# VectorE's order in a conv input stage: taps written out by hand, two blocks by turns, thirteen blocks in place of twelve

## The chip, the cores and the metric

The kernel runs on one core of one Trainium2 chip. The metric is the device time of one execution in microseconds. Before the change the median of three executions is 1987.35 us (1987.07 to 1987.43).

## The reference

A trunk of four residual layers over 256 tokens of 2048 features: a causal convolution module, an MLP, a state-space layer, an MLP, and a last RMSNorm. The change touches the first layer alone, up to its LayerNorm:

```
u = rms_norm(x, g) @ w_in + b_in              # (256, 2048) @ (2048, 4096)
a, gate = split(u)
v = a * sigmoid(gate)                         # (256, 2048)
v = depthwise_conv(v, dw, 31 taps, causal) + dw_b
v = silu(layer_norm(v, ln_g, ln_b))           # mean and variance over the 2048 channels
x = x + v @ w_out + b_out
```

## The kernel before

**Layout.** In this stage channels lie on the 128 partitions and the 256 tokens along the free axis. The 2048 channels are 16 blocks of 128, numbered 0 to 15. For each block the loop in `conv_in` multiplies the 2048 input features by the block's 128 value columns and 128 gate columns.

**Matmuls.** Float32 operands are split in a high and a low part. Each weight piece (512 KB, a quarter of a block) is loaded, cast to its high part `hi` on ScalarE (L118), and its low part `lo` is a subtraction (L125), on VectorE for blocks 0 and 1 and on GpSimd for the others (`pool_lo`). `mm_g` then issues 24 matmuls of 256 columns for the quarter (L211 to L213), so a block is 96. `hi` and `lo` have four buffers each: the cast of a quarter waits until TensorE is done with the quarter four before. The accumulators `acc` have two buffers: block c+2 can start when block c's gate is done.

**The gate** (`gate`, L446 to L448), with raised priority: VectorE multiplies the accumulator by the RMSNorm factor (L446, "the gate's multiplication" below), ScalarE takes the sigmoid into `ga` (L447), VectorE forms `(a + b) * ga` into `vT` (L448, "the gate's second instruction").

**The convolution of 31 taps** has two forms.

- Blocks 0 to 11 (`depthwise`): ScalarE computes the first tap into a PSUM bank `cv` (L527), then VectorE adds 30 taps, each one instruction of 128x256 (L829), the last one into `vT`. A tap needs the tap of its block before it. Such a row of taps is called a chain below.
- Blocks 12 to 15, the packed ones (`depthwise_packed`): TensorE does the taps with 32 small matmuls (`pk`, L484) over `R`, a copy of the block shifted four ways. For 12 to 14 ScalarE's queue writes `vT` to DRAM (`vd`) and loads `R` back; for 15 the shifted copies are made by eight copies on VectorE (L470) and eight on ScalarE (L468). VectorE then adds bias and shift (`finish`, L829 `vT<-pk,vecs,shift`). Blocks 12 and 13 run eight quarters after their gates, 14 and 15 after the last block of the stage, in a tail that holds everything up to the first matmul of `conv_out` (L222).

**LayerNorm sums.** Column sums by small matmuls into one bank `stat` (L539). When the first four blocks are convolved, their mean becomes `shift` (a matmul into the bank `mean`, L560, and a VectorE instruction, L562). `centre` then subtracts `shift` from four blocks at once (VectorE, L569, 128x1024) and squares them (ScalarE, L571).

**Banks.** The pool `ms` has four PSUM banks: `cv` of the running chains, `stat`, `mean`, and one in two of the packed sums.

**What sets the order.** A scheduler in the build places the instructions on the five engines, by their place in the program, raised priorities, and its own idea of when operands are ready. On the chip each engine runs its own list strictly in order. `behind(x)` makes the scheduler place one instruction after another. `after(n, f)` calls f some n quarters later. Before the change the taps have no such tie: the scheduler mixes the chains and the gates.

**Beside the stage** GpSimd also builds the packed weights (`wpk`, L386) and adds the output bias to x (L400), for which it loads `bo` itself (L398).

Of the kernel before, what the change touches and what calls it, by code (L numbers as in the profile page):

```python
# [12 lines left out]
AF = mybir.ActivationFunctionType  # L13
ALU = mybir.AluOpType
# [4 lines left out]
P = 128  # L19
EPS = 1e-6  # L20
D = 2048
T = 256
# [7 lines left out]
VW = PAD + T + 2  # L30
NQ = 4
EARLY = 4
PACKED = (12, 13, 14, 15)
URGENT = 300


class Trunk:
# [72 lines left out]
    def split(self, h, urgent=True):  # L110
        i, half = divmod(h, 2)
        raw = self.raws[i] if half == 0 else self.raws.pop(i)
        nk = raw.shape[1] // 2
        sl = raw[:, half * nk:(half + 1) * nk]
        hi = self.w.tile([P, nk] + list(raw.shape[2:]), F32R, tag="hi", name="hi", bufs=4)
        lo = self.w.tile([P, nk] + list(raw.shape[2:]), F32R, tag="lo", name="lo", bufs=4)
        with self.tc.high_priority(offset=URGENT if urgent else 0):
            self.nc.scalar.activation(hi, sl, AF.Copy)  # L118
            eng = self.nc.gpsimd if i in self.pool_lo else self.nc.vector
            if self.barrier is not None and h == 2 * self.barrier + 2:  # L120
                self.low_late = lambda: eng.tensor_tensor(out=lo, in0=sl, in1=hi.bitcast(F32), op=ALU.subtract)
                self.parts[h] = (hi, lo)
                return None
            with self.behind(self.lo_gate) if self.lo_gate is not None else nullcontext():
                ins = eng.tensor_tensor(out=lo, in0=sl, in1=hi.bitcast(F32), op=ALU.subtract)  # L125
            self.lo_gate = None
            if i in self.pool_lo:
                self.pool_ins = ins
            else:
                self.lo_ins = ins  # L130
        self.parts[h] = (hi, lo)
        return ins
# [278 lines left out]
    def conv_in(self):  # L411
        w = self.a["conv_w_in"][0].rearrange("(k p) (h c) -> p k h c", p=P, h=2)
        self.fed = set()
        self.tail = []
        self.stat = None
        st = {}
        for c in range(KB):
            for kc in range(2):
                def consume(hi, lo, half, c=c, kc=kc):
                    if kc == 0 and half == 0:  # L420
                        st["acc"] = self.acc2()
                    A = st["acc"][:, :, 0:T]
                    hi, lo = (t.rearrange("p k h c -> p k (h c)") for t in (hi, lo))
                    self.mm_g([A[:, 0], A[:, 1]], self.hT, hi, lo, kc * 8 + half * 4,
                              kc == 0 and half == 0, kc == 1 and half == 1)
                    if kc == 1 and half == 1:
                        self.gate(c, A)
                if c >= 2:
                    self.pool_lo.add(len(self.steps))
                self.add(w[:, kc * 8:(kc + 1) * 8, :, c * P:(c + 1) * P], [P, 8, 2, P], consume)  # L430
# [10 lines left out]
    def gate(self, c, A):  # L441
        nc = self.nc
        b_in = self.vec("b_in")
        t = self.tmp.tile([P, T], F32, tag="ga", name="ga", bufs=2)
        with self.tc.high_priority(offset=URGENT):
            nc.vector.tensor_tensor(out=A, in0=A, in1=self.rstdB.broadcast_to([P, 2, T]), op=ALU.mult)  # L446
            nc.scalar.activation(t, A[:, 1, :], AF.Sigmoid, bias=b_in[:, KB + c:KB + c + 1])  # L447
            nc.vector.scalar_tensor_tensor(out=self.cblk(c), in0=A[:, 0, :], scalar=b_in[:, c:c + 1], in1=t,  # L448
                                           op0=ALU.add, op1=ALU.mult)
        if c in PACKED:  # L450
            self.depthwise_packed(c)
        else:
            self.depthwise(c)

    def depthwise_packed(self, c):

# [4 lines left out]
        if last:  # L461
            for g in range(4):
                for r in range(4):
                    o = R[32 * r:32 * r + 32, g, :]
                    v = self.vb(c)[32 * g:32 * g + 32, r:r + T + 28]
                    with self.tc.high_priority(offset=URGENT):
                        if r % 2:
                            nc.scalar.activation(o, v, AF.Copy)  # L468
                        else:
                            nc.vector.tensor_copy(out=o, in_=v)  # L470
        else:
            vd = self.dram.tile([P, VW], F32, name=f"vd{i}")
            nc.scalar.dma_start(out=vd, in_=self.vb(c))

            def fetch():
                for r in range(4):
                    nc.scalar.dma_start(out=R[32 * r:32 * r + 32],
                                        in_=vd.rearrange("(g c) t -> c g t", g=4)[:, :, r:r + T + 28])
            self.after(1, fetch)
# [17 lines left out]
                self.colsum(self.stat[:, h, :], (c,), lambda i: v, h == 0)  # L497

        def run():
            ps = self.acc2(f"pk{c}")[:, 0, 0:T] if i % 2 else self.bank([P, T], name=f"pk{c}")  # L500
            products(ps, 0, 5)
            if i:
                feed(c - 1)
# [4 lines left out]
                    self.warm = nc.scalar.activation(warm, R[:, 0, 0:1], AF.Silu)  # L508
            products(ps, 5, 8)
            finish(ps)  # L510
        if i < 2:
            self.after(8, run)
        elif not last:
            self.tail.append(run)
        else:
            while self.pending:
                self.tick()
            for f in self.tail:
                f()
            run()  # L520

    def depthwise(self, c):

        tap = lambda j: (self.vb(c)[:, j:j + T], self.dw[:, c, j:j + 1])
        acc = self.bank([P, T], name="cv")
        v, w = tap(0)
        self.nc.scalar.activation(acc, v, AF.Identity, scale=w, bias=self.vec("dw_b")[:, c:c + 1])  # L527
        for j in range(1, TAPS):
            v, w = tap(j)
            self.stt(self.cblk(c) if j == TAPS - 1 else acc, v, w, acc, ALU.mult, ALU.add)  # L530
        self.ln_feed(c)

# [7 lines left out]
    def ln_feed(self, c):  # L542
        self.fed.add(c)
        if self.stat is None:
            self.stat = self.bank([P, 2, T], name="stat")
        g = range(c // 4 * 4, c // 4 * 4 + 4)
        if not all(i in self.fed for i in g):
            return
        if c < EARLY:
            self.colsum(self.stat[:, 0, :], g, lambda i: self.cblk(g[i]), True)  # L550
            self.after(2, self.ln_shift)
        else:
            self.after(2, lambda: self.centre(g[0], 4))

    def ln_shift(self):
        nc = self.nc
# [2 lines left out]
        ps = self.bank([P, T], name="mean")  # L559
        nc.tensor.matmul(ps, lhsT=self.q4, rhs=t, start=True, stop=True)  # L560
        self.shift = self.const.tile([P, T], F32, name="shift")
        nc.vector.tensor_scalar(out=self.shift, in0=ps, scalar1=1.0 / (EARLY * P), scalar2=None, op0=ALU.mult)  # L562
        for c in range(0, EARLY, 4):
            self.centre(c, 4)

    def centre(self, c, n):
        nc = self.nc
        v = self.cblks(c, n)
        nc.vector.tensor_tensor(out=v, in0=v, in1=self.shift.unsqueeze(1).broadcast_to([P, n, T]), op=ALU.subtract)  # L569
        sq = self.t4([P, n, T], name="sq")  # L570
        nc.scalar.activation(sq, v, AF.Square)  # L571
        cs = range(c, c + n)
# [1035 lines left out]
```

## Time and profile before

| | |
|---|---|
| median of 3 executions | 1987.35 us |
| the profiled execution's own time | 1987.61 us |
| its span, first to last instruction | 1985.8 us |
| TensorE busy | 1966.9 us, 99% |
| VectorE busy | 1401.3 us, 71% |
| ScalarE busy | 952.4 us, 48% |
| GpSimd busy | 274.8 us, 14% |
| the chain that ended last | TensorE 96%, VectorE 2%, DMA 1% |
| mean granted TensorE clock | 0.999 |

Shares are averages over the whole program; the change lies in the first 232 us. Matmuls overlap, so a matmul's duration (0.28 us) is longer than the distance from one to the next. VectorE's instructions overlap too: a tap lasts 0.48 us and the next starts 0.39 us after it.

### The profile page before, as it was taken

Reading aid. Unit: us, or ns where it says so; the run is one execution under the profiler, and the core shown is the slowest. Engines: PE = TensorE matmul, PEld = TensorE weight load, DVE = VectorE, ACT = ScalarE, POOL = GpSimd, SP = SyncE. Lnnn points to the kernel's source line nnn. Section 1 sums busy time; section 2 is a strip of 40 time slices with the busy share of each in tenths; the row PEclk is TensorE's granted clock in tenths of the full one; section 3 lists DMA queues with packets and bytes.
Section 4 is the critical chain, followed back from the end, with each engine's and each line's share of the span. In section 5 each row is a group of like instructions: output and inputs, shape, how many; then the busy total and the mean of one; then the engine's idle time right before and its main releaser. Section 6 shows DMA issues by size and latency. Waiting matters only on the chain.

```text
span 1985.8 us, 28885 instructions
## 1 busy us (share of the span) xinstructions
PE 1966.9 (99%) x11604; PEld 1687.0 (85%) x11604; DVE 1401.3 (71%) x1904; ACT 952.4 (48%) x1179; POOL 274.8 (14%) x252
## 2 busy tenths in 40 slices
PE   8999999999999999999999999999999999999998
PEld 8999788888888888888888788888888888888887
DVE  6899798888787777777558847565555565555655
ACT  6443655544444544444445445454444454444444
POOL 3998300000000221222010000000000000000000
PEclk9999999999999999999999999999999999999999
DMA  8767458667686877877898865665666656565653
GB/s 228 190 184 207 147 183 267 206 226 245 200 260 192 214 229 253 265 246 238 319 308 298 304 215 186 191 191 189 193 190 192 190 191 191 190 213 190 192 191 128
DMA packets 317030, 428.49 MB, mean 216 GB/s; under 512 B 9761, under 2 KB 211553, under 8 KB 313537
## 3 DMA queue, kind: packets, MB, share of 16 engines
q1 hardware_dynamic: 300976, 384.59, 61.6%
q0 software_dynamic: 12352, 37.49, 6.3%
q10 hardware_dynamic: 3568, 4.56, 0.8%
q8 instruction: 91, 1.49, 0.3%
q14 instruction: 43, 0.35, 0.1%
HBM read 400.08 MB, written 34.91 MB: 219 GB/s over the span
## 4 chain that ended last, share of the span: by engine, by line
PE 96%; DVE 2%; DMA 1%; issue 0%; SPq 0%; POOL 0%; ACT 0%; POOLq 0%; DVEq 0%; ACTq 0%
PE acc L199 24%; PE acc L222 15%; PE acc L223 15%; PE acc L224 15%; PE acc L202 12%; PE acc L213 3%; PE acc L212 3%; PE acc L211 3%; PE pk L484 1%; DMA Vt<-Vd 0%; SPq L92 0%; PE kp L1113 0%; PE xw L1254 0%; DMA raw<-in_conv_w_in_dram 0%; PE xt L254 0%
## 5 line engine op out<-in xcount | busy, mean ns | idle before, releaser
L118 ACT ACTIVATE hi<-raw 128x1024 fp32r<-128x1024 f32 x672 | 711.6, 1060 | 953.5 <-PE acc L224 510.2
L125 DVE TENSOR_TENSOR lo<-raw,hi 128x1024 fp32r<-128x1024 f32 x611 | 747.9, 1226 | 505.6 <-ACT hi L118 501.3
L199 PE MATMUL acc<-hT,hi 128*128 128x512 f32 x2048 | 514.4, 393 | 0.0
L199 PEld LDWEIGHTS acc<-hT,hi 128*128 128x128 f32 x2048 | 368.9, 189 | 68.0 <-issue 1.6
L222 PE MATMUL acc<-hi,rT 128*128 128x512 f32 x992 | 387.2, 391 | 0.0
L223 PE MATMUL acc<-lo,rT 128*128 128x512 f32 x992 | 386.4, 390 | 0.0
L224 PE MATMUL acc<-hi,rT 128*128 128x512 f32 x992 | 386.0, 389 | 0.0
L202 PEld LDWEIGHTS acc<-hT,lo 128*128 128x128 f32 x2048 | 279.6, 190 | 20.0
L202 PE MATMUL acc<-hT,lo 128*128 128x256 f32 x2048 | 286.3, 282 | 0.0
L222 PEld LDWEIGHTS acc<-hi,rT 128*128 128x128 f32 x992 | 186.3, 188 | 39.6 <-issue 1.6
L224 PEld LDWEIGHTS acc<-hi,rT 128*128 128x128 f32 x992 | 186.3, 188 | 39.1
L223 PEld LDWEIGHTS acc<-lo,rT 128*128 128x128 f32 x992 | 186.3, 188 | 38.0 <-issue 0.2
L125 POOL TENSOR_TENSOR lo<-raw,hi 128x1024 fp32r<-128x1024 f32 x60 | 143.1, 2402 | 31.3 <-ACT hi L118 24.8
L211 PE MATMUL acc<-hT,hi 128*128 128x256 f32 x512 | 146.1, 286 | 0.9 <-ACT hi L118 0.9
L212 PE MATMUL acc<-hT,hi 128*128 128x256 f32 x512 | 145.7, 286 | 0.3 <-DVE hT L259 0.3
L213 PE MATMUL acc<-hT,lo 128*128 128x256 f32 x512 | 145.5, 286 | 0.0
L829 DVE SCALAR_TENSOR_TENSOR cv<-vT,dw,cv 128x256 f32<-128x256 f32 x348 | 141.3, 486 | 2.2 <-ACT cv L527 1.7
L820 DVE TENSOR_TENSOR x<-x,acc 128x1024 f32<-128x1024 f32 (+1 forms) x72 | 83.6, 1161 | 27.6 <-PE acc L224 22.0
L211 PEld LDWEIGHTS acc<-hT,hi 128*128 128x128 f32 x512 | 98.9, 193 | 3.0 <-issue 1.6
L222 PE MATMUL acc<-hi,yT 128*128 128x512 f32 x256 | 101.1, 395 | 0.0
L212 PEld LDWEIGHTS acc<-hT,hi 128*128 128x128 f32 x512 | 98.8, 193 | 2.2 <-issue 1.6
L223 PE MATMUL acc<-lo,yT 128*128 128x512 f32 x256 | 99.9, 390 | 0.6 <-DVE lo L125 0.6
(285 smaller groups left out, 1722.9 us busy)
## 6 DMA issues: line engine op xcount, KB each, us to landing
raw<-in_mlp_w_up_dram SPq DMA_DIRECT2D x128, 1024.0 KB, 5.8
raw<-in_mlp_w_down_dram SPq DMA_DIRECT2D x128, 1024.0 KB, 5.2
raw<-in_ssm_w_glu_dram SPq DMA_DIRECT2D x32, 1024.0 KB, 5.5
raw<-in_conv_w_in_dram SPq DMA_DIRECT2D x60, 512.0 KB, 5.6
raw<-in_conv_w_out_dram SPq DMA_DIRECT2D x16, 1024.0 KB, 5.2
Vd<-bv POOLq DMA_DIRECT2D x16, 512.0 KB, 6.3
Md<-Kd POOLq DMA_DIRECT2D x32, 256.0 KB, 7.2
Wt<-Wd SPq DMA_DIRECT2D x8, 1024.0 KB, 10.1
```

Source lines behind the costliest of these rows:

```text
L118: self.nc.scalar.activation(hi, sl, AF.Copy)
L125: ins = eng.tensor_tensor(out=lo, in0=sl, in1=hi.bitcast(F32), op=ALU.subtract)
L199: mm(accs[m], lhsT=hi[:, kk, cs[m]], rhs=xT(k0 + kk), start=first and kk == 0, stop=False)
L202: mm(accs[m][:, 0:T], lhsT=lo[:, kk, cs[m]], rhs=xT(k0 + kk)[:, 0, :], start=False, stop=last and kk == 3)
L211: mm(accs[m], lhsT=hi[:, kk, c], rhs=x[:, 0, :], start=first and kk == 0, stop=False)
L212: mm(accs[m], lhsT=hi[:, kk, c], rhs=x[:, 1, :], start=False, stop=False)
L213: mm(accs[m], lhsT=lo[:, kk, c], rhs=x[:, 0, :], start=False, stop=last and kk == 3)
L222: mm(acc[:, b, :], lhsT=ak[:, 0, t], rhs=hi[:, kk, :], start=first and kk == 0, stop=False)
L223: mm(acc[:, b, :], lhsT=ak[:, 0, t], rhs=lo[:, kk, :], start=False, stop=False)
L224: self.mm_last = mm(acc[:, b, :], lhsT=ak[:, 1, t], rhs=hi[:, kk, :], start=False, stop=last and kk == 1)
L820: return self.nc.vector.tensor_tensor(out=out, in0=a, in1=b, op=op)
L829: return self.nc.vector.scalar_tensor_tensor(out=out, in0=a, scalar=s, in1=b, op0=op0, op1=op1)
```

## The change

Five things are done:

- The packed blocks are 13, 14 and 15; block 12 becomes a chain of 30 taps. Block 13 runs six quarters after its gate, 14 and 15 in the tail.
- All VectorE instructions of gates, taps, `shift`, `centre` and the copies for block 15 are issued through `dve`, which places each behind the one before: VectorE's order is now the order of the program. `taps(n)` issues n taps, by turns from the two oldest chains. From the last but one quarter of block 1 on there are 7 taps after a quarter, and in a block's last quarter 4, the gate's multiplication, 3, and the gate's second instruction.
- Up to three chains are open (two while block 3's runs); ScalarE's first tap is issued when a chain is opened.
- On ScalarE the next cast `hi` is placed behind the gate's sigmoid and, where a chain is opened, behind its first tap (`act_first`).
- The mean's matmul is issued one quarter after its sums, and `shift` and `centre` two quarters after that; the later `centre` calls come at once.

```
-PACKED = (12, 13, 14, 15)
+PACKED = (13, 14, 15)
...
         with self.tc.high_priority(offset=URGENT if urgent else 0):
-            self.nc.scalar.activation(hi, sl, AF.Copy)
+            with self.behind(self.act_first) if self.act_first is not None else nullcontext():
+                self.nc.scalar.activation(hi, sl, AF.Copy)
+            self.act_first = None
...
                     if kc == 1 and half == 1:
                         self.gate(c, A)
+                    h = 4 * c + 2 * kc + half
+                    if h >= 6 and c < KB - 1:
+                        self.taps(4 if kc == 1 and half == 1 else 7)
+                    elif c == KB - 1 and not (kc == 1 and half == 1):
+                        self.taps(7)
...
-            nc.vector.tensor_tensor(out=A, in0=A, in1=self.rstdB.broadcast_to([P, 2, T]), op=ALU.mult)
-            nc.scalar.activation(t, A[:, 1, :], AF.Sigmoid, bias=b_in[:, KB + c:KB + c + 1])
-            nc.vector.scalar_tensor_tensor(out=self.cblk(c), in0=A[:, 0, :], scalar=b_in[:, c:c + 1], in1=t,
-                                           op0=ALU.add, op1=ALU.mult)
+            self.dve(lambda: nc.vector.tensor_tensor(out=A, in0=A, in1=self.rstdB.broadcast_to([P, 2, T]), op=ALU.mult))
+            self.act_first = nc.scalar.activation(t, A[:, 1, :], AF.Sigmoid, bias=b_in[:, KB + c:KB + c + 1])
+        self.taps(3)
+        with self.tc.high_priority(offset=URGENT):
+            self.dve(lambda: nc.vector.scalar_tensor_tensor(out=self.cblk(c), in0=A[:, 0, :], scalar=b_in[:, c:c + 1], in1=t,
+                                                            op0=ALU.add, op1=ALU.mult))
         if c in PACKED:
             self.depthwise_packed(c)
         else:
-            self.depthwise(c)
+            self.waiting.append(c)
+            self.begin_chains()
+
+    def dve(self, fn):
+
+        with self.behind(self.dv) if self.dv is not None else nullcontext():
+            self.dv = fn()
+
+    def begin_chains(self):
+
+        while self.waiting and len(self.chains) < (2 if any(x[0] == EARLY - 1 for x in self.chains) else 3):
+            c = self.waiting.pop(0)
+            acc = self.bank([P, T], name="cv")
+            self.act_first = self.nc.scalar.activation(acc, self.vb(c)[:, 0:T], AF.Identity, scale=self.dw[:, c, 0:1],
+                                                       bias=self.vec("dw_b")[:, c:c + 1])
+            self.chains.append([c, acc, 1])
+
+    def taps(self, n):
+        for _ in range(n):
+            if not self.chains:
+                return
+            self.turn = (self.turn + 1) % min(2, len(self.chains))
+            x = self.chains[self.turn]
+            c, acc, j = x
+            last = j == TAPS - 1
+            self.dve(lambda: self.stt(self.cblk(c) if last else acc, self.vb(c)[:, j:j + T], self.dw[:, c, j:j + 1], acc,
+                                      ALU.mult, ALU.add))
+            x[2] += 1
+            if last:
+                self.chains.remove(x)
+                self.ln_feed(c)
+                self.begin_chains()
...
-        if i < 2:
-            self.after(8, run)
+        if i == 0:
+            self.after(6, run)
...
-        g = range(c // 4 * 4, c // 4 * 4 + 4)
+        g = range(c // 4 * 4, min(c // 4 * 4 + 4, PACKED[0]))
...
-            self.after(2, self.ln_shift)
+            self.after(1, self.ln_shift)
         else:
-            self.after(2, lambda: self.centre(g[0], 4))
+            self.centre(g[0], len(g))
...
-        nc.vector.tensor_scalar(out=self.shift, in0=ps, scalar1=1.0 / (EARLY * P), scalar2=None, op0=ALU.mult)
-        for c in range(0, EARLY, 4):
-            self.centre(c, 4)
+
+        def use():
+            self.dve(lambda: nc.vector.tensor_scalar(out=self.shift, in0=ps, scalar1=1.0 / (EARLY * P), scalar2=None,
+                                                     op0=ALU.mult))
+            self.centre(0, EARLY)
+        self.after(2, use)
```

From `conv_out` on, the order of every engine is the same in both programs. Three places in the stage follow.

**VectorE, the end of the stage.** Before: from block 14's gate (first row, the multiplication) to block 15's gate and the first copies for its packed form.

```order
L446 TENSOR_TENSOR acc<-acc,bcs 128x2x256
L829 SCALAR_TENSOR_TENSOR cv<-vT,dw,cv 128x256 x3
L448 SCALAR_TENSOR_TENSOR vT<-acc,vecs,ga 128x256
L829 SCALAR_TENSOR_TENSOR cv<-vT,dw,cv 128x256 x20
L829 SCALAR_TENSOR_TENSOR vT<-vT,dw,cv 128x256
L829 SCALAR_TENSOR_TENSOR cv<-vT,dw,cv 128x256
L829 SCALAR_TENSOR_TENSOR vT<-vT,dw,cv 128x256
L569 TENSOR_TENSOR vT<-vT,shift 128x4x256
L829 SCALAR_TENSOR_TENSOR vT<-pk_2723,vecs,shift 128x256
L446 TENSOR_TENSOR acc<-acc,bcs 128x2x256
```

Now, from the end of block 11's chain (first row) to block 15's gate (last row); `pk_2649` is block 13's packed sum, and the taps behind the first row are all of block 12's chain.

```order
L864 SCALAR_TENSOR_TENSOR vT<-vT,dw,cv 128x256
L603 TENSOR_TENSOR vT<-vT,shift 128x4x256
L864 SCALAR_TENSOR_TENSOR cv<-vT,dw,cv 128x256
L454 TENSOR_TENSOR acc<-acc,bcs 128x2x256
L864 SCALAR_TENSOR_TENSOR cv<-vT,dw,cv 128x256 x3
L458 SCALAR_TENSOR_TENSOR vT<-acc,vecs,ga 128x256
L864 SCALAR_TENSOR_TENSOR cv<-vT,dw,cv 128x256 x8
L864 SCALAR_TENSOR_TENSOR vT<-pk_2649,vecs,shift 128x256
L864 SCALAR_TENSOR_TENSOR cv<-vT,dw,cv 128x256 x7
L864 SCALAR_TENSOR_TENSOR vT<-vT,dw,cv 128x256
L603 TENSOR_TENSOR vT<-vT,shift 128x256
L454 TENSOR_TENSOR acc<-acc,bcs 128x2x256
```

Before, `centre` of blocks 8 to 11 and the packed sum were the last things ahead of block 15's gate; now eight taps, a second `centre` and, ahead of them, the instruction that reads `pk_2649` stand there.

**ScalarE, around the first gate.** Before: the casts of quarters 6 to 9, the sigmoid `ga` of block 0 with its table load, the first tap of chain 0, sixteen small copies `dp`, two casts, the sigmoid of block 1.

```order
L118 ACTIVATE hi<-raw 128x1024 x4
L447 ACT_TABLE_LOAD
L447 ACTIVATE ga<-acc,vecs 128x256
L527 ACTIVATE cv<-vT,vecs,dw 128x256
L379 ACTIVATE dp<-dw 32x4x8 x16
L118 ACTIVATE hi<-raw 128x1024 x2
L447 ACTIVATE ga<-acc,vecs 128x256
```

Now the same stretch, from the cast of quarter 6:

```order
L119 ACTIVATE hi<-raw 128x1024
L455 ACT_TABLE_LOAD
L455 ACTIVATE ga<-acc,vecs 128x256
L476 ACTIVATE cv<-vT,vecs,dw 128x256
L119 ACTIVATE hi<-raw 128x1024 x3
L381 ACTIVATE dp<-dw 32x3x8 x10
L119 ACTIVATE hi<-raw 128x1024
L381 ACTIVATE dp<-dw 32x3x8 x6
L455 ACTIVATE ga<-acc,vecs 128x256
```

The cast of quarter 7 and the ones behind it now stand behind the first gate's sigmoid and the first tap; the second sigmoid stands behind the small copies as before.

**TensorE, the last quarter of block 15.** Before, the packed sum of block 13 stood between the third quarter (first row) and the last one.

```order
L213 MATMUL acc<-hT,lo 128x256
L484 MATMUL pk_2723<-R,wpk 32x256 x32
L211 MATMUL acc<-hT,hi 128x256
L212 MATMUL acc<-hT,hi 128x256
```

Now:

```order
L215 MATMUL acc<-hT,lo 128x256
L570 MATMUL stat<-vT,ones 32x256 x4
L570 MATMUL stat<-sq,ones 32x256 x4
L213 MATMUL acc<-hT,hi 128x256
L214 MATMUL acc<-hT,hi 128x256
L526 MATMUL pk_2649<-R,wpk 32x256 x32
L215 MATMUL acc<-hT,lo 128x256
```

The column sums of blocks 8 to 11, which were in the tail, now stand ahead of that packed sum, and the packed sum of block 12 is gone from block 14.

## Rows read from the trace of the kernel before

**Rows 1.** The page: its first line, and VectorE's share of the low parts.

```profile
span 1985.8 us, 28885 instructions
...
L125 DVE TENSOR_TENSOR lo<-raw,hi 128x1024 fp32r<-128x1024 f32 x611 | 747.9, 1226 | 505.6 <-ACT hi L118 501.3
```

**Rows 2.** Windows: stretch, length, busy us of PE, PEld, DVE, ACT, POOL; clock; DMA.

```profile
140.00:160.00 20.00, 20.00 (x168) 19.93 (x168) 20.00 (x52) 9.77 (x13) 20.00 (x10) 1.00 0.66 182
160.00:214.40 54.40, 54.40 (x526) 49.68 (x524) 51.59 (x121) 21.68 (x26) 41.77 (x18) 1.00 0.81 225
214.40:231.80 17.40, 16.75 (x203) 12.50 (x203) 10.47 (x23) 9.65 (x21) 6.67 (x8) 1.00 0.36 116
```

**Rows 3.** VectorE by groups, 40 to 214.4 us: busy, mean ns, idle before.

```profile
L829 DVE SCALAR_TENSOR_TENSOR cv<-vT,dw,cv 128x256 f32<-128x256 f32 x342 | 138.3, 486 | 1.3 <-ACT cv L527 1.0
L446 DVE TENSOR_TENSOR acc<-acc,bcs 128x512 f32<-128x512 f32 x13 | 9.1, 698 | 7.3 <-PE acc L213 7.2
```

**Rows 4.** VectorE's timeline: start, length in us, instructions, idle before and its releaser.

```profile
36.25 3.11 DVE L829 SCALAR_TENSOR_TENSOR cv<-vT,dw,cv 128x256 f32<-128x256 f32 x6 [0.70 <-ACT cv L527]
39.27 0.69 DVE L446 TENSOR_TENSOR acc<-acc,bcs 128x512 f32<-128x512 f32 x1
39.88 1.00 DVE L829 SCALAR_TENSOR_TENSOR cv<-vT,dw,cv 128x256 f32<-128x256 f32 x2
42.86 0.48 DVE L448 SCALAR_TENSOR_TENSOR vT<-acc,vecs,ga 128x256 f32<-128x256 f32 x1 [1.98 <-ACT ga L447]
...
105.17 1.68 DVE L569 TENSOR_TENSOR vT<-vT,shift 128x1024 f32<-128x1024 f32 x1
...
127.18 11.84 DVE L829 SCALAR_TENSOR_TENSOR cv<-vT,dw,cv 128x256 f32<-128x256 f32 x30
...
178.91 2.41 DVE L569 TENSOR_TENSOR vT<-vT,shift 128x1024 f32<-128x1024 f32 x1
...
210.63 1.74 DVE L569 TENSOR_TENSOR vT<-vT,shift 128x1024 f32<-128x1024 f32 x1
...
214.49 0.70 DVE L446 TENSOR_TENSOR acc<-acc,bcs 128x512 f32<-128x512 f32 x1 [1.73 <-PE acc L213]
```

**Rows 5.** TensorE's timeline: four column sums, block 12's packed sum.

```profile
183.96 0.64 PE L539 MATMUL stat<-vT,ones 128*32 128x256 f32 x8
...
192.42 3.66 PE L484 MATMUL pk<-R,wpk 128*32 128x256 f32 x64
```

**Rows 6.** ScalarE's timeline around the first two gates.

```profile
32.69 1.28 ACT L447 ACT_TABLE_LOAD   x1
33.98 0.47 ACT L447 ACTIVATE ga<-acc,vecs 128x256 f32<-128x256 f32 x1
35.65 0.57 ACT L527 ACTIVATE cv<-vT,vecs,dw 128x256 f32<-128x256 f32 x1 [1.19 <-DVE dw L355]
36.16 4.28 ACT L379 ACTIVATE dp<-dw 32x32 f32<-32x32 f32 x16
...
43.89 1.04 ACT L118 ACTIVATE hi<-raw 128x1024 fp32r<-128x1024 f32 x1
```

**Rows 7.** GpSimd by groups, 40 to 214.4 us, and landing of `bo`.

```profile
L125 POOL TENSOR_TENSOR lo<-raw,hi 128x1024 fp32r<-128x1024 f32 x57 | 136.0, 2403 | 20.6 <-ACT hi L118 20.5
L400 POOL TENSOR_TENSOR x<-x,bo 128x1024 f32<-128x1024 f32 x4 | 9.6, 2391 | 0.0
...
DMA to landing us min/median/max: 3.4/4.0/5.0
```

**Rows 8.** Timelines in the tail: block 15's copies on VectorE, conv_out's first matmul.

```profile
216.41 3.89 DVE L470 COPY R<-vT 32x284 f32<-32x284 f32 x8
...
231.80 0.50 PE L222 MATMUL acc<-hi,sT 128*128 128x512 f32 x1 [0.25 <-ACT sT L237]
```

**Rows 9.** Windows behind the program's last matmul: columns as in rows 2.

```profile
1978.10:1982.80 4.70, 0.00 (x0) 0.00 (x0) 2.29 (x7) 1.17 (x3) 0.56 (x1) 1.00 0.94 346
1982.80:1985.80 3.00, 0.00 (x0) 0.00 (x0) 0.00 (x0) 0.00 (x0) 0.00 (x0) 0.50 0.42 156
```

More of the change, by code (lines that the diff above doesn't have):

```diff
@@ L414, in conv_in @@
         self.tail = []
-        self.stat = None
+        self.stat = self.dv = self.act_first = None
+        self.waiting, self.chains, self.turn = [], [], 0
         st = {}
@@ L469, in depthwise_packed @@
                         else:
-                            nc.vector.tensor_copy(out=o, in_=v)
+                            self.dve(lambda: nc.vector.tensor_copy(out=o, in_=v))
+            self.taps(TAPS * KB)
         else:
@@ L499, in run @@
         def run():
-            ps = self.acc2(f"pk{c}")[:, 0, 0:T] if i % 2 else self.bank([P, T], name=f"pk{c}")
+            ps = self.acc2(f"pk{c}")[:, 0, 0:T] if c % 2 else self.bank([P, T], name=f"pk{c}")
             products(ps, 0, 5)
@@ L520, in depthwise_packed @@
             run()
[L522 to L531, printed above, removed]
     def colsum(self, out, cs, src, first):
@@ L568, in centre @@
         v = self.cblks(c, n)
-        nc.vector.tensor_tensor(out=v, in0=v, in1=self.shift.unsqueeze(1).broadcast_to([P, n, T]), op=ALU.subtract)
+        self.dve(lambda: nc.vector.tensor_tensor(out=v, in0=v, in1=self.shift.unsqueeze(1).broadcast_to([P, n, T]),
+                                                 op=ALU.subtract))
         sq = self.t4([P, n, T], name="sq")
```

## The prediction

> **What bounds the kernel now.** I read the page first: the span [rows 1] is a TensorE span. Then the windows of the stage, to see how much room each engine has [rows 2]. TensorE has no idle time up to the last gate, at a granted clock of 1.00; from 140 to 160 us it issues 168 matmuls in 20 us, 0.119 us each, so the 96 of a block take 11.4 to 11.5 us and a quarter 2.9. In the same window VectorE and GpSimd are 100% busy as well. VectorE is thus not far from being the bound itself. Its groups say the same: its idle time is 7.3 us before the 13 gate multiplications, nearly all waiting for TensorE, and hardly anything before taps [rows 3]. The last such wait is 1.73 us, before the last gate at 214.49 us [rows 4]. The tail from there to conv_out's first matmul lasts 231.80 - 214.49 = 17.3 us; it is a chain from that gate over block 15's copies, which end at about 220.3 us, to the packed sum of block 15 [rows 2, 8]. So the stage ends 17.3 us after block 15's gate multiplication, and the question is when that one comes. Call it G15.
>
> **What goes away.** Block 12's packed sum takes 3.66 us of TensorE [rows 5], and TensorE is the bound. If nothing else became late, G15 would come 3.66 us sooner. The addition that reads that sum goes from VectorE too, 0.4 us (a tap's 0.48 less the overlap).
>
> **What is added: VectorE's list, added up.** The new order is fixed, so its time without any wait can be summed from the second gate's multiplication (G1) to G15.
>
> - A tap that alternates with another chain: 30 in 11.84 us, (11.84 - 0.48)/29 = 0.392 us each [rows 4]. A tap of a chain alone waits for itself: 6 in 3.11 us, (3.11 - 0.48)/5 = 0.525 us [rows 4].
> - There are 13 x 30 = 390 taps. Seven stand ahead of G1. Of the other 383, 23 are alone: three of chain 0 behind G1, and the last 20 of block 12, since chains 11 and 12 are the last two and chain 12 has only had 10 taps when 11 ends. 360 x 0.392 = 141.1 us, 23 x 0.525 = 12.1 us.
> - 14 gates (1 to 14), multiplication 39.88 - 39.27 = 0.61 us and second instruction 0.40 us: 14.1 us [rows 4].
> - Three `centre` of four blocks, at the times of before, 1.6 + 2.3 + 1.7 = 5.6 us (1.68, 2.41 and 1.74 less the overlap) [rows 4]. `shift`, the one-block `centre` and the addition behind block 13's packed sum: 0.4 us each, as a tap without overlap, 1.2 us.
>
> Sum 174.1 us. The Trainium skill has a rule on the three `centre`: SBUF, State Buffer, "Who interferes with whom", says that a VectorE instruction with two SBUF inputs contends with a GpSimd instruction that reads SBUF, and one with a single SBUF input does not. The trace agrees: taps keep 0.392 us beside a GpSimd that is 100% busy, and one of three `centre` took 2.41 us. If all three met GpSimd so, the sum would be 1.4 us more.
>
> G1 itself moves. The sigmoid's table load no longer stands behind two casts, which brings the first tap forward by some 1.4 us, from 36.25 to 34.9 us (the load's 1.28 us, 32.69 to 33.98 [rows 6], now runs ahead of the operands). Behind it come seven lone taps, 3.7 us, where six stood, then the low part of quarter 7, which was done before, 1.1 us [rows 1], and three small set-up instructions, 0.7 us together (estimate: the nearest row is the 0.48 us of a tap, half each). G1 = 34.9 + 3.7 + 1.1 + 0.7 = 40.4 us, against 39.27. Then G15 is at least 40.4 + 174.1 = **214.5 us, where it is now**. The 30 added taps eat all of VectorE's idle time and all of the 3.66 us. TensorE's gain is hidden behind VectorE; what is left to ask is how long VectorE's fixed list waits.
>
> **The waits in the new list.**
>
> - Second gate. The sigmoid of block 1 stands behind four casts (1.0 us each) and sixteen small copies (4.28 us) [rows 6]: 34.9 + 4.0 + 4.3 = 43.2, done at 43.7 us. VectorE is there at 40.4 + 0.6 + 1.6 = 42.6. Wait 1.1 us, then 0.7 us for the new chain's first tap, as at 36.25 us [rows 4]. Before, 1.98 us were lost here too, but in slack. Total **1.8** us (0.7 to 2.5).
> - Quarter 31. GpSimd now issues two loads of `bo` directly ahead of the addition that needs one, and the low part of quarter 31 stands behind it: 4.0 us landing, 2.4 addition, 2.4 low part, 8.8 us [rows 7], where TensorE takes 2.9 us a quarter. TensorE idles some 2.5 us in block 7. It was ahead of VectorE by about that, so VectorE's next gate waits only **0.2** us (0 to 2.5).
> - Block 13's packed sum. VectorE's addition of it stands ahead of eight more taps, the second `centre` and G15. VectorE reaches it 0.6 + 1.6 + 0.4 + 8 x 0.525 = 6.8 us after G14. TensorE has it after block 14, three quarters (8.6), eight column sums (1.3, twice 0.64 [rows 5]), two matmuls and 3.66 us: 13.8 us. How far VectorE's G14 lies behind TensorE's end of block 14 decides. TensorE can't run far ahead: each block's fourth quarter is cast behind the gate before it and the first tap of a new chain. From a gate: 2.3 us to the end of the second instruction, 0.6 first tap [rows 6], 1.05 cast [rows 6], 2.4 low part [rows 7], 2.9 the quarter: 9.3 us. The last chain is opened at gate 12, so block 13 ends at G12 + 9.3 or later, block 14 at + 20.8. VectorE takes 12.0 us for a block (28 taps and a gate) and 13.6 with a `centre`: G14 = G12 + 25.6. The lag is 4.8 us, and the wait 13.8 - 4.8 - 6.8 = **2.2** us (0 to 4: a lag of 7, or of 3).
>
> Sum 4.2 us; G15 = 218.7, 4.2 us later than before. The tail behind it is the same list (the same 16 copies, block 15's sum, LayerNorm), so 17.3 us; block 14's packed sum still lies beside the copies. ScalarE's copies now stand behind a cast of 1.05 us, which costs 0 to 0.5 us, since before a cast stood just ahead of the sigmoid; I take 0.1. Everything later is a TensorE list without gaps, in the same order, and shifts as a whole.
>
> **Sum.** Against the profiled execution's own 1987.61 us: + 4.3 = 1991.9. That execution is 0.26 us above the median of 1987.35, so the forecast is **1991.7 us**.
>
> **Rivals.**
>
> - *VectorE's list runs without the waits.* If the sigmoid comes in time, `bo` is early and the lag is 7 us, G15 stays at 214.5 to 215: 1987.5 us. For it: before, taps waited 1.3 us in all the stage [rows 3]. Against: ScalarE's order at the second gate is plain. Chance 0.22.
> - *TensorE stays the bound and the 3.66 us are kept*: 1983.7 us. This needs VectorE's 174 us to be 4 us too large, from the point where a tap falls below 0.381 us (360 taps). 0.392 us is the distance of taps that wait for nothing, beside the same neighbours, so I see no room. Chance 0.07. This is the case on the other side.
> - *TensorE's clock falls in the new idle time.* Behind the program's last matmul the clock was granted at 1.00 for 4.7 us and at 0.50, the lower level, after that [rows 9]. TensorE now idles in block 7 and, between block 14's packed sum and the end of block 15's copies, for some us. If the clock falls there, block 15's sum and the LayerNorm's matmuls run at half speed: + 3.66 us or a little more, 1996 us. The Trainium skill ("TensorE: Matmul & The Clock Gate", Part 1, "What's actually happening") has it so: throttled is the default state, and only activity releases it. The row agrees as far as it goes; no row shows a fall inside the stage, as TensorE never idles there. Chance 0.10.
>
> **How the numbers follow.** The forecast's mechanism, VectorE the bound with some of its waits, has 0.61. Its own range is 1989.5 to 1995: the waits' bounds are 0.7 to 9 us in all, and all three small or all three large at once is unlikely. About 0.2% (4 us) is what a measurement of this kernel can tell from no change, so the limits are 1983.4 and 1991.3 us. Of the forecast's 0.61 some 0.45 lie above 1991.3 and 0.16 below; the clock rival adds 0.10 to slower; the rival without waits adds 0.22 to the same, and the last one gives 0.03 to the same and 0.04 to faster. Slower 0.55, same 0.41, faster 0.04. Range for 8 in 10: 1987.2 (the rival without waits lies at its lower end) to 1996.3 (the clock).
>
> **What would show it.** In the new profile VectorE should have next to no idle time from 45 us to block 15's gate, except before the addition of block 13's packed sum (about 2 us, for TensorE), and 12.0 us from one gate to the next. TensorE should show gaps that end with a low part or a cast, above all in block 7, where before there is none; the gate multiplication of block 15 should start at about 218.7 us, and conv_out's first matmul 17.3 us later. I am wrong if VectorE waits for TensorE at the gates as before (TensorE is the bound), if a tap takes less than 0.392 us, if G15 is at 215 or earlier, or if the tail is longer than 18 us or shows a clock below 1.00.

## The result, and the profile after

The changed kernel takes 1993.43 us (median of 8 executions, 1993.04 to 1994.86) against 1987.57 us for the kernel before beside it: ratio 1.0028, 95% interval 1.0020 to 1.0037. It is slower by 5.9 us. The forecast was 1991.7 us, range 1987.2 to 1996.3, with slower as the likeliest sign. The profiled execution took 1993.38 us.

The first group answers to [rows 1] and [rows 2]: the page's first line, then windows from 140 us to the last gate, the tail (from there to conv_out's first matmul), and a part of the tail. Columns as in [rows 2].

```profile
span 1991.6 us, 28764 instructions
```

```profile
140.00:160.00 20.00, 20.00 (x173) 18.91 (x172) 19.97 (x49) 9.79 (x12) 18.91 (x8) 1.00 0.72 198
160.00:217.70 57.70, 56.62 (x523) 53.74 (x525) 54.33 (x131) 21.44 (x26) 45.87 (x20) 1.00 0.74 205
217.70:237.70 20.00, 15.91 (x174) 12.47 (x165) 11.23 (x24) 10.06 (x22) 6.53 (x8) 0.91 0.31 112
225.90:229.32 3.42, 3.42 (x38) 2.67 (x30) 0.00 (x0) 0.67 (x2) 0.00 (x0) 0.50 0.35 127
```

The span is 5.8 us longer. In the tail TensorE is busy for 15.9 of 20.0 us, where it had 16.8 of 17.4, and the clock is 0.91, because it was granted at 0.50, the lower level, for 3.4 us.

VectorE by groups from 40 to 217.7 us, as in [rows 3], with all groups that waited:

```profile
L864 DVE SCALAR_TENSOR_TENSOR cv<-vT,dw,cv 128x256 f32<-128x256 f32 x373 | 151.8, 488 | 1.3 <-ACT cv L476 0.6
L454 DVE TENSOR_TENSOR acc<-acc,bcs 128x512 f32<-128x512 f32 x14 | 9.7, 695 | 0.0
...
L603 DVE TENSOR_TENSOR vT<-vT,shift 128x1024 f32<-128x1024 f32 (+1 forms) x4 | 5.3, 1325 | 0.1
L864 DVE SCALAR_TENSOR_TENSOR vT<-pk,vecs,shift 128x256 f32<-128x256 f32 x1 | 0.5, 485 | 2.7 <-PE pk L526 2.7
L595 DVE TENSOR_SCALAR shift<-mean 128x256 f32<-128x256 f32 x1 | 0.4, 426 | 0.6 <-PE mean L591 0.6
```

The 14 gate multiplications waited 0.0 us; before it was 7.3. VectorE no longer waits for TensorE at the gates. It waits for TensorE at two places only, 2.7 us at the packed sum of block 13 and 0.6 at the mean behind `shift`. Its timeline around the places of [rows 4]: the second gate (41.09) and the first tap of the chain opened there, two gates in mid-stage, and the end.

```profile
37.67 1.53 DVE L931 COPY rowsel<-dtau 128x128 f32<-128x128 f32 x1
...
41.09 0.69 DVE L454 TENSOR_TENSOR acc<-acc,bcs 128x512 f32<-128x512 f32 x1
...
44.24 2.05 DVE L864 SCALAR_TENSOR_TENSOR cv<-vT,dw,cv 128x256 f32<-128x256 f32 x5 [0.64 <-ACT cv L476]
...
117.30 0.69 DVE L454 TENSOR_TENSOR acc<-acc,bcs 128x512 f32<-128x512 f32 x1
...
129.26 0.69 DVE L454 TENSOR_TENSOR acc<-acc,bcs 128x512 f32<-128x512 f32 x1
...
212.88 0.48 DVE L864 SCALAR_TENSOR_TENSOR vT<-pk,vecs,shift 128x256 f32<-128x256 f32 x1 [2.74 <-PE pk L526]
213.28 3.63 DVE L864 SCALAR_TENSOR_TENSOR cv<-vT,dw,cv 128x256 f32<-128x256 f32 x7
...
217.81 0.69 DVE L454 TENSOR_TENSOR acc<-acc,bcs 128x512 f32<-128x512 f32 x1
...
219.56 4.54 DVE L511 COPY R<-vT 32x284 f32<-32x284 f32 x8
```

From gate to gate VectorE takes 129.26 - 117.30 = 11.96 us, 12.0 as forecast. G15 is at 217.81 us, 3.3 us later than in [rows 4]. TensorE's timeline, which answers to [rows 5] and [rows 8]: its last matmul of block 15, then the tail.

```profile
215.35 0.28 PE L215 MATMUL acc<-hT,lo 128*128 128x256 f32 x1
216.71 3.66 PE L526 MATMUL pk<-R,wpk 128*32 128x256 f32 x64 [1.08 <-DMA R<-vd]
...
224.68 0.40 PE L570 MATMUL stat<-vT,ones 128*32 128x256 f32 x1 [3.45 <-DVE vT L864]
...
224.99 4.07 PE L526 MATMUL pk<-R,wpk 128*32 128x256 f32 x41
...
237.71 0.50 PE L224 MATMUL acc<-hi,sT 128*128 128x512 f32 x1 [0.25 <-ACT sT L239]
```

TensorE ends block 15 at 215.6 us and VectorE multiplies it 2.2 us later; before, that followed within 0.1 us. TensorE then idles 1.08 and 3.45 us, and from 1.2 us behind the end of the second gap, 225.9 us, the clock is at 0.50. The tail is 237.71 - 217.81 = 19.9 us, against 17.3. So the 5.9 us are 3.3 ahead of G15 and 2.6 behind it.

### The profile page after: what moved, and what is told of

Read it like the earlier page. It is cut to its first block, busy times and chain, and to the rows that moved or that the text cites. A ratio compares the mean times of both kernels' runs of the same rounds, so it can differ in the third digit from the quotient of the medians.

```text
span 1991.6 us, 28764 instructions
## 1 busy us (share of the span) xinstructions
PE 1965.5 (99%) x11540; PEld 1686.6 (85%) x11540; DVE 1412.9 (71%) x1934; ACT 950.4 (48%) x1180; POOL 273.5 (14%) x251
## 4 chain that ended last, share of the span: by engine, by line
PE 86%; DVE 1%; DMA 0%; issue 0%; ACT 0%; POOL 0%; SPq 0%; POOLq 0%; DVEq 0%
PE acc L201 24%; PE acc L224 15%; PE acc L225 15%; PE acc L226 15%; PE acc L204 12%; DMA Vt<-Vd 0%; PE kp L1148 0%; PE xw L1289 0%; PE xt L256 0%; PE acc L235 0%; PE acc L234 0%; PE acc L236 0%; PE mv L1381 0%; DVE S L855 0%; DVE lo L127 0%
## 5 line engine op out<-in xcount | busy, mean ns | idle before, releaser
L201 PEld LDWEIGHTS acc<-hT,hi 128*128 128x128 f32 x2048 | 368.9, 189 | 68.0 <-issue 1.2
L204 PEld LDWEIGHTS acc<-hT,lo 128*128 128x128 f32 x2048 | 279.6, 190 | 20.0
L864 DVE SCALAR_TENSOR_TENSOR cv<-vT,dw,cv 128x256 f32<-128x256 f32 x377 | 153.8, 488 | 2.1 <-ACT cv L476 1.3
L215 PEld LDWEIGHTS acc<-hT,lo 128*128 128x128 f32 x512 | 98.1, 193 | 6.0 <-POOL lo L127 3.9
L213 PEld LDWEIGHTS acc<-hT,hi 128*128 128x128 f32 x512 | 98.8, 193 | 3.4 <-ACT hi L119 2.1
```

The costliest lines, as they stand in the source:

```text
L201: mm(accs[m], lhsT=hi[:, kk, cs[m]], rhs=xT(k0 + kk), start=first and kk == 0, stop=False)
L204: mm(accs[m][:, 0:T], lhsT=lo[:, kk, cs[m]], rhs=xT(k0 + kk)[:, 0, :], start=False, stop=last and kk == 3)
L213: mm(accs[m], lhsT=hi[:, kk, c], rhs=x[:, 0, :], start=first and kk == 0, stop=False)
L215: mm(accs[m], lhsT=lo[:, kk, c], rhs=x[:, 0, :], start=False, stop=last and kk == 3)
L864: return self.nc.vector.scalar_tensor_tensor(out=out, in0=a, scalar=s, in1=b, op0=op0, op1=op1)
```

## Experiments

Theory A: VectorE's list is the bound up to G15, with its wait at block 13's packed sum; theory C: the clock makes most of the longer tail. Rival B: the written-out order as such holds TensorE back. All ratios are against the kernel before.

**e3: the addition of block 13's packed sum goes behind the last taps.** In `run`, for block 13 alone (the addition itself joins VectorE's written list):

```diff
...
-            finish(ps)
+            if i == 0:
+                self.after(2, lambda: finish(ps))     # VectorE's list: ... taps, centre, this, gate 15
+            else:
+                finish(ps)
```

> The changed kernel with VectorE's addition of block 13's packed sum moved from ahead of the last taps to directly ahead of block 15's gate. Theory A: VectorE's wait of 2.74 us goes, its list ends at 215.2 us, TensorE ends block 15 at 215.6, so block 15's gate moves from 217.8 to 215.7 us: 1991.3, and if TensorE's idle time in the tail, then 1.3 us in place of 3.45, no longer brings the clock down, 1989.6. Rival B (TensorE's gaps bound the stage): no change, 1993.4.

Measured: 1989.89 us, ratio 1.0012 (1.0003 to 1.0021); the profiled execution 1989.41.

```profile
205.88 7.83 DVE L868 SCALAR_TENSOR_TENSOR cv<-vT,dw,cv 128x256 f32<-128x256 f32 x15
...
214.26 1.14 DVE L607 TENSOR_TENSOR vT<-vT,shift 128x256 f32<-128x256 f32 x1
215.31 0.47 DVE L868 SCALAR_TENSOR_TENSOR vT<-pk,vecs,shift 128x256 f32<-128x256 f32 x1
215.71 0.70 DVE L454 TENSOR_TENSOR acc<-acc,bcs 128x512 f32<-128x512 f32 x1
```

The wait is gone, G15 is at 215.71 as A has it, and TensorE's idle pieces in the tail are 1.29 and 1.14 us at a clock of 1.00; the tail is 18.25 us. One instruction's place in VectorE's list was worth 2.1 us ahead of G15 and, through the clock, 1.65 behind it.

**e4: twelve small matmuls in TensorE's gap of 3.45 us**, in `run` of block 15, behind the column sums of block 13:

```diff
...
+            if last:
+                self.keep_warm(12, self.fed_ins, ps[:, 0:P])
             products(ps, 0, 5)
```

> The changed kernel with twelve matmuls of 128x128 put on TensorE behind block 14's packed sum, in the 3.45 us in which it idles in the tail. Theory C (the 3.41 us at half the clock behind that gap cost 1.7 of the tail's 2.6 us): the clock stays at 1.00 to conv_out, the tail falls from 19.9 to 18.2 us, 1991.7. Rival D (the tail is longer by the idle time and the copies alone): no change, 1993.4.

Measured: 1992.54 us, ratio 1.0026 (1.0015 to 1.0037). TensorE in the tail (the twelve matmuls stand as 24 records, as the 32 of a packed sum stand as 64), and a window of the stretch that ran at 0.50 in the changed kernel:

```profile
221.32 2.94 PE L191 MATMUL pk<-ident 128*128 128x128 f32 x24
224.53 0.40 PE L573 MATMUL stat<-vT,ones 128*32 128x256 f32 x1 [0.26 <-DVE vT L868]
...
224.78 2.57 PE L526 MATMUL pk<-R,wpk 128*32 128x256 f32 x41
```

```profile
225.80:229.20 3.40, 3.40 (x53) 1.90 (x44) 0.53 (x2) 1.01 (x3) 0.00 (x0) 1.00 0.39 135
```

G15 is where it was, block 15's packed sum begins at the same distance from it, and its 41 records take 2.57 in place of 4.07 us. The tail is 18.23 us, 1.67 shorter: theory C holds. The medians (1992.54 and 1993.43) show 0.89 of it. The profiled e4, 1993.9 us, lost 2.3 us behind conv_out's first matmul against the changed kernel, 1.6 of them at a half-clock stretch of its own (last section); what its median execution lost there no trace shows.

**e1: block 12 packed again, the written-out order kept** (`PACKED = (12, 13, 14, 15)`, both early packed sums six quarters behind their gates).

> The changed kernel with block 12 packed again (four packed blocks, twelve chains), everything else of the change kept: tap order written out, two blocks by turns. Theory A (VectorE's list with thirteen chains is what bounds the stage): thirty taps, some 12 to 15 us, leave VectorE; it waits for TensorE at the gates again, TensorE takes its 3.66 us back, block 15's gate multiplication is at 214.5 to 216 us and the time at 1987.5 to 1990. Rival B (the written-out order itself costs TensorE its 3.4 us of gaps): the gaps stay, TensorE is 3.66 us longer, block 15's gate is at 218 us or later and the time at 1991 to 1994.

Measured: 1997.41 us, ratio 1.0046 (1.0033 to 1.0059). Theory A as I stated it fell; the time lies above rival B's range too. The gates up to block 9 keep the changed kernel's times within 0.3 us:

```profile
117.53 0.69 DVE L454 TENSOR_TENSOR acc<-acc,bcs 128x512 f32<-128x512 f32 x1
...
129.49 0.68 DVE L454 TENSOR_TENSOR acc<-acc,bcs 128x512 f32<-128x512 f32 x1
...
203.68 3.48 DVE L603 TENSOR_TENSOR vT<-vT,shift 128x1024 f32<-128x1024 f32 x1
...
222.06 0.70 DVE L454 TENSOR_TENSOR acc<-acc,bcs 128x512 f32<-128x512 f32 x1 [6.85 <-PE acc L215]
```

The order puts 28 taps between two gates whatever the number of chains: again 11.96 us a block, more than TensorE's 11.5. From block 10 on two `centre` of 3.10 and 3.48 us make them later still. VectorE then runs out of taps and waits 6.85 us at the end. So it is not the 13th chain in itself that sets the pace, but the number of taps written between two gates.

**e5 and e11: four packed blocks and 26 taps from gate to gate.** e11 also puts the packed sums of 12 and 13 eight quarters behind their gates.

```diff
-                        self.taps(4 if kc == 1 and half == 1 else 7)
+                        self.taps(4 if kc == 1 and half == 1 else 6 if kc or half else 7)
...
-            self.after(6, run)
+            self.after(8, run)          # e11, and behind the last quarter's matmuls
```

> Four packed blocks and the written-out order as in e1, but 26 taps from gate to gate in place of 28. Theory A2 (the number of taps written between two gates sets the pace: 28 x 0.392 + 1.0 = 12.0 us a block is more than TensorE's 11.5, 26 x 0.392 + 1.0 = 11.2 is less): VectorE waits for TensorE at the gates, TensorE is not held back, block 15's gate falls from 222.1 us in e1 to 215 to 217.5 us, and the time from 1997.4 to 1989 to 1992. Rival B2 (the fixed order and the casts behind sigmoid and first tap hold TensorE back whatever the pace): the gate stays at 220 us or later, 1995 or more.

> e5 (four packed blocks, written-out order, 26 taps from gate to gate) with the packed sums of blocks 12 and 13 placed as in the kernel before, eight quarters behind their gates, in place of six, and behind the quarter issued last. Theory A2 with P: TensorE does not stand in order behind a packed sum whose data are late (4.4 us in e5); if each `centre` meets one instruction of GpSimd at most, block 13 ends on TensorE at 184.4 us, block 15's gate is at 215 to 217 us and the time 1988.5 to 1991, much less than e1's 1997.4. If `centre` stands behind four again, 8.5 us more, 1997 to 1999.5. Rival B2 (written order and cast rule hold TensorE back in any case): 1995 or more with no long `centre`.

Measured: e5 2006.99 us, ratio 1.0098 (1.0084 to 1.0111); e11 2000.64, 1.0066 (1.0053 to 1.0078). Up to block 10 A2 holds: G10 is at 148.9 and 148.6 us (149.3 before, 154.5 after the change). Then, in e5, on VectorE, on GpSimd and on TensorE:

```profile
153.55 9.68 DVE L603 TENSOR_TENSOR vT<-vT,shift 128x1024 f32<-128x1024 f32 x1
...
152.79 2.40 POOL L402 TENSOR_TENSOR x<-x,bo 128x1024 f32<-128x1024 f32 x1
155.16 6.99 POOL L127 TENSOR_TENSOR lo<-raw,hi 128x1024 fp32r<-128x1024 f32 x3
...
163.29 1.08 PE L570 MATMUL stat<-vT,ones 128*32 128x256 f32 x8 [5.78 <-DVE vT L603]
```

One `centre` took 9.68 us (9.69 in e11). It ends 1.1 us after the last of four GpSimd instructions, which ran without a pause. The column sums behind it stood on TensorE for 5.78 us.

**e9 and e12: e5 and e11 with one operand of `centre` in PSUM.** The instruction subtracts the bank of sums, not the shift; only times count here.

```diff
-        ... in0=v, in1=self.shift.unsqueeze(1).broadcast_to([P, n, T])
+        ... in0=v, in1=self.stat[:, 0:1, :].broadcast_to([P, n, T])
```

> e5 with one operand changed: the instruction `centre` subtracts the bank of sums in PSUM in place of the shift in SBUF (a wrong value, so LayerNorm's input is not the reference's; sizes and order are the same). Theory P (`centre`, with both inputs in SBUF, stands still while GpSimd works and starts only when GpSimd's instruction ends): each `centre` takes 1.1 to 1.3 us, the one of 9.68 us in e5 too, TensorE does not idle 5.8 us behind it, and with 26 taps from gate to gate block 15's gate is at 215 to 220 us, 1989 to 1995. Rival Q (it stood still for another reason, such as its own data): 9 us again, 2005 or more.

> The same as e11 with `centre` subtracting the bank of sums in PSUM (LayerNorm's input not the reference's), so that it does not meet GpSimd. Theory A2: block 13 ends on TensorE at 184.4 us as in e9, block 15's gate at 215 to 216.5 us, 1988.5 to 1990.5. Rival B2: 1995 or more.

Measured: e9 1997.91 us, ratio 1.0051 (1.0039 to 1.0064); e12 1991.46, 1.0022 (1.0013 to 1.0031). In e9, `centre` and what GpSimd did beside it:

```profile
153.18 1.22 DVE L603 TENSOR_TENSOR vT<-vT,stat 128x1024 f32<-128x1024 f32 x1
...
152.42 2.40 POOL L402 TENSOR_TENSOR x<-x,bo 128x1024 f32<-128x1024 f32 x1
```

All `centre` of four blocks take 1.21 or 1.22 us in both; beside three of the six GpSimd was at work, as here: theory P holds. e9's time is above its range because TensorE still stood 4.50 us in order behind block 12's packed sum, whose data were late; e12, with that mended, tells what the written order costs without either accident. VectorE by groups, 40 to 217.3 us:

```profile
L454 DVE TENSOR_TENSOR acc<-acc,bcs 128x512 f32<-128x512 f32 x14 | 9.8, 697 | 6.3 <-PE acc L215 6.3
```

It waits for TensorE at the gates as before the change, so TensorE is the bound again; yet G15 is at 217.4 us, above the 215 to 216.5 expected, and the time 1 us above its range. In my count I had left out that the column sums of blocks 8 to 11, and two of block 12, now run on TensorE ahead of G15; besides, TensorE idled 0.84 us at 75 us, waiting for a low part. Rival B is right to that extent: this order costs TensorE some 2.9 us (217.36 - 214.49) even at the right pace.

**e2: the kernel before with three packed blocks**, the scheduler's order kept.

> The kernel before with three packed blocks in place of four and nothing else: the scheduler sets the order of the taps. Theory A: TensorE loses 3.66 us, so block 15's gate comes at about 211 us, but the thirty added taps are left over and stand behind it, among the copies: VectorE works without idle time until its instruction on stat at about 221 to 223 us, the tail is 5 to 9 us longer than the 17.3 of before, and the time is 1985 to 1992, no gain of 3.66. Rival B (only the written order is at fault): the gain is kept, 1983.9.

Measured: 1999.21 us, ratio 1.0052 (1.0039 to 1.0064). Block 15's gate, a long row of taps behind it, and TensorE and its clock:

```profile
210.04 0.70 DVE L446 TENSOR_TENSOR acc<-acc,bcs 128x512 f32<-128x512 f32 x1 [0.20 <-PE acc L213]
...
216.72 7.52 DVE L829 SCALAR_TENSOR_TENSOR cv<-vT,dw,cv 128x256 f32<-128x256 f32 x19
...
216.94 1.51 PE L484 MATMUL pk<-R,wpk 128*32 128x256 f32 x12 [6.94 <-DVE R L470]
```

```profile
217.00:222.00 5.00, 5.00 (x48) 2.63 (x52) 5.00 (x14) 0.00 (x0) 0.00 (x0) 0.50 0.25 91
```

TensorE's gain reaches the gate (214.49 - 210.04 = 4.45 us sooner), and is lost behind it: left-over taps run to 229 us, TensorE idles 6.94 us, the clock falls, and the tail is 30.9 us. My range was 7 us too low: I had VectorE done at 221 to 223 us and left out its 9.3 us of waiting at the gates, which remained. Of the two ways to have thirteen chains the written order is the cheaper one.

**e6 and e8: the cast rule taken out** (casts no longer behind sigmoid and first tap), block 13's addition in the tail; e8 with even turns (e7) as well.

> The changed kernel without the rule that a cast stands behind the sigmoid and the first tap, and with the addition of block 13's packed sum behind block 15's copies (the scheduler then puts that packed sum behind block 15's matmuls). Theory A: TensorE loses its gaps of 3 us and ends block 15 near 211 us, yet VectorE's list sets block 15's gate: 217.8 - 2.74 - 0.4 = 214.7 us, and with a tail of 18 us the time is 1988.5, from 1987.5 to 1989.5. Rival B: with TensorE's gaps gone the gate comes at 212 us or earlier, 1985.5 or less.

> e6 and e7 together: casts free, addition of block 13's packed sum behind the copies, last chains in turn. Theory A: both bounds are lifted, block 15's gate at 212 us; the packed sum of block 14 then waits for its data (on TensorE at 216.7 us so far) and the tail is 18 to 20 us: conv_out at 230 to 232 us, 1986 to 1988, no slower than before. Rival F (the gate moves but block 14's data hold the tail where it was): 1988.5 to 1990.

Measured: e6 1998.06 us, ratio 1.0053 (1.0041 to 1.0066); e8 1998.65, 1.0055 (1.0043 to 1.0068). Both missed. In e6, VectorE's longest wait for the sigmoid, and ScalarE there:

```profile
96.21 0.48 DVE L457 SCALAR_TENSOR_TENSOR vT<-acc,vecs,ga 128x256 f32<-128x256 f32 x1 [3.37 <-ACT ga L454]
...
94.75 1.06 ACT L118 ACTIVATE hi<-raw 128x1024 fp32r<-128x1024 f32 x1 [2.54 <-PE acc L213]
95.72 0.46 ACT L454 ACTIVATE ga<-acc,vecs 128x256 f32<-128x256 f32 x1
```

The sigmoid stands behind a cast that waits until TensorE frees its buffer. VectorE lost 8.4 us at five such gates. The rule is no cost of the change; it protects the list that bounds it.

**e7 and e10: e3 with even turns** (from block 12's start on, the chain with most taps left goes next, never the same one twice running); e10 with `centre` on the PSUM operand as well, its value again not the shift.

> e3 (addition of block 13's packed sum directly ahead of block 15's gate) and the last chains taken in turn by what is left of them, so that block 12's last twenty taps no longer wait each for itself: VectorE's list is 20 x (0.525 - 0.392) = 2.7 us shorter. Theory A says that TensorE is the next bound, at 214.3 to 215.7 us: block 15's gate follows its matmuls without lag, and the time is 1988.5 to 1990, hardly less than e3's 1989.9. Rival E (VectorE still the bound in e3): the gate at 213.0 us, 1987.2.

> e7 with the same change of one operand (LayerNorm's input again not the reference's). Theory P: the four `centre` take 1.2, 1.2, 1.2 and 0.4 us in place of 2.43, 1.24, 2.25 and 2.09, VectorE's list is 3.9 us shorter, and block 15's gate follows TensorE's matmuls without lag, at 214.3 us in place of 216.0: 1987.6, at most 1988.3. Rival Q: no change, 1989.3.

Measured: e7 1989.34 us, ratio 1.0009 (1.0000 to 1.0018), within A's range but not for A's reason; e10 1996.06, 1.0042 (1.0028 to 1.0056). In e7 TensorE ended block 15 at 214.26 us, and yet G15 came at 215.98:

```profile
210.90 2.25 DVE L610 TENSOR_TENSOR vT<-vT,shift 128x1024 f32<-128x1024 f32 x1
...
213.57 2.09 DVE L610 TENSOR_TENSOR vT<-vT,shift 128x256 f32<-128x256 f32 x1
```

The taps were to give 2.7 us. Against e3, the two `centre` that met GpSimd took 2.0 of it back (2.25 for 1.23, 2.09 for 1.14), and a wait for the first tap of block 12's chain 0.64. What e7 gains on e3 at conv_out's first matmul, 0.5 us, it gains in the tail (17.46 us for 18.25). In e10 three `centre` take 1.21 to 1.22 us and the last one 0.42, but that last one now needs the sums, which TensorE had placed late, and waited 6.10 us for them: the durations bear P out, and the time says nothing of it. e7 is the fastest version with three packed blocks, 4.1 us below the changed kernel. None beat the kernel before.

## Why the prediction was right, point by point

- **The bound moves to VectorE: right.** No wait at the gates, 11.96 us from gate to gate, a lag of 1 us or more behind TensorE at every block; shown by e3, where 2.74 us taken off VectorE's list moved G15 by 2.1, until TensorE's end of block 15.
- **G1: 41.1 in place of 40.4 us.** The set-up instructions that I priced at 0.7 together contain a copy, `rowsel`, that took 0.21 us before, next to an idle GpSimd. Now it stands among the lone taps and took 1.53 us (37.67 above): it ends 0.1 us after a low part on GpSimd.

  Before:

```profile
30.98 0.21 DVE L896 COPY rowsel<-dtau 128x128 f32<-128x128 f32 x1
```

  and GpSimd's low part now:

```profile
36.63 2.50 POOL L127 TENSOR_TENSOR lo<-raw,hi 128x1024 fp32r<-128x1024 f32 x1 [11.87 <-ACT hi L119]
```

- **The list without waits: 172.8 us in place of 174.1** (217.81 - 41.09 = 176.7, less 4.0 of waits). The taps are as priced. The three `centre`, taken over from [rows 4] at 5.6 us, took 2.40, 1.24 and 1.23: their length is set by where GpSimd stands, not by their work.
- **The waits: 4.0 in place of 4.2 us, with other parts.** Block 13's packed sum 2.74 (2.2 forecast); the second gate 0.64, the new chain's first tap alone (1.8 forecast; the sigmoid was in time); the wait for `mean` 0.58, which I had not named; `bo` nothing. TensorE's gap in block 7, forecast at some 2.5 us, was 0.65; its longest ahead of the end of block 15 was 1.29 us, at 76.6 us.
- **The tail: this step failed.** I wrote that it is the same list and so 17.3 + 0.1 us; it was 19.9, with a clock below 1.00, both signs that I had named for being wrong. VectorE's list was the same, but TensorE was ahead of it by 2.2 us, no longer had the column sums of blocks 8 to 11 to do there, and idled. e4 gives 1.67 of the 2.6 us to the clock. The other 0.9 the traces place. One of VectorE's eight copies lasts 2.36 us, before one lasted 1.69, the others 0.30. Both end 0.16 us after a low part on GpSimd; before:

```profile
215.57 2.37 POOL L125 TENSOR_TENSOR lo<-raw,hi 128x1024 fp32r<-128x1024 f32 x1 [4.29 <-ACT hi L118]
...
216.41 1.69 DVE L470 COPY R<-vT 32x284 f32<-32x284 f32 x1
```

  and now:

```profile
220.03 2.35 POOL L127 TENSOR_TENSOR lo<-raw,hi 128x1024 fp32r<-128x1024 f32 x1 [4.80 <-ACT hi L119]
...
220.18 2.36 DVE L511 COPY R<-vT 32x284 f32<-32x284 f32 x1
```

  So the copies end 6.3 us behind G15 in place of 5.8. From there to conv_out e4, at full clock, takes 11.9 us in place of 11.5: block 15's packed sum begins 0.6 to 0.7 us behind the last copy, because TensorE's order has a column sum ahead of it that waits for VectorE's addition of block 14's packed sum (224.68 above). Before, TensorE did not idle there and began it at 220.1 us, before the last copy ended; in e7, where that column sum stands later, this part takes 11.0 us.
- **The clock rival came true, beside the forecast's mechanism and not in its place.** It was put at the right spot, between block 14's packed sum and the end of block 15's copies. Its price of 3.66 us or more was too high: half the clock for 3.4 us cost 1.7. Forecast and rival together are 1991.7 + 1.7 = 1993.4, the time measured; but that is luck: the forecast was too late by 0.9 at G15, and the tail's other 0.9 made it good.
- **TensorE keeps its 3.66 us: wrong, as argued.** e2 shows them at the gate and gone behind it.

## What to carry to other kernels

An order written by hand has a pace of its own: count the work between two points where engines meet against the other engine's time for the same stretch, since a surplus of 0.5 us a block takes away any slack that a scheduler's order left there. When a list becomes the bound, put every instruction that waits for another engine as late in it as its reader allows: one such move was worth 3.7 of the 5.9 us here (3.5 by the medians). And look at what the engine that is no longer the bound does in its new idle time: TensorE's clock is part of that price. Where VectorE's list is the bound, look also at what GpSimd does beside it: three of the prediction's misses, at G1, in the `centre` and in the copies, are VectorE instructions that stood still for GpSimd, before the change or after it.

## What the runs showed of the hardware

- **Two kinds of VectorE instruction stood still while a GpSimd subtraction or addition was at work: `centre`, with both inputs in SBUF, and a copy from SBUF to SBUF, with one.** `centre` of four blocks takes 1.22 us with one operand in PSUM and 1.23 next to an idle GpSimd. Otherwise it ends 1.1 us behind GpSimd's instruction: 2.40, and behind four in a row 9.68 us. [rows 4] had this in its 1.68, 2.41 and 1.74, which I read as a price. One of block 15's eight copies lasts 1.69 to 2.39 us in 11 of the 14 kernels and ends 0.16 us behind GpSimd's instruction; in e2, e6 and e8, with none on GpSimd there, all take 0.30. Taps, whose accumulator is in PSUM, kept their pace. The Trainium skill (SBUF — State Buffer, "Who interferes with whom") calls the shared port pair an exclusive lock; the traces agree, and add that VectorE's turn need not come when GpSimd's instruction ends. The prediction's short form of that section's rule, that a single SBUF input does not contend, left out its condition "outside the 2-port perf modes", and the copies show that without it the rule is too wide.
- **A gap of 3.45 us on TensorE was followed, 1.2 us after its end, by 3.41 us at half the clock; in e3 gaps of 1.29 and 1.14 us were not. The length of a gap does not settle it.** In e1's tail gaps of 0.96 and 0.92 us were followed by 3.41 us at half the clock, from 229.65 us on, and the tail is 19.93 us; in e12 the same two gaps were not, and it is 18.25. A gap of 1.50 us near 1066 to 1070 us, in the state-space layer, was followed by 1.00 in the kernel before and by half-clock in e4, where the window behind it shows 0.69 and TensorE took 7.0 us in place of 5.4 to the next matmuls of 512 columns:

```profile
1070.00:1075.00 5.00, 4.45 (x97) 3.79 (x97) 4.91 (x9) 1.25 (x3) 0.00 (x0) 0.69 1.02 423
```
